# A hybrid decoder layer on one core: the mixer's steps are recorded in another order

## The chip, the core and the metric

The kernel runs on one core of a Trainium2 chip. A core has a matrix engine (TensorE, PE in the profile; its weight loads are PEld), three engines for elementwise work (VectorE or DVE, ScalarE or ACT, GpSimd or POOL) and a queue that issues transfers (SyncE or SP). Each engine works through its own instruction queue in order; semaphores tie the queues together. The metric is the time of one execution on the device in microseconds.

## What is computed

One decoder layer on a sequence of 512 tokens with 1024 features, all in float32: half a gated feed-forward step (2816 hidden), a mixer of windowed attention (16 query heads, 2 key heads, 64 each, window 128) and a 31-tap depthwise convolution, another half feed-forward step, and a gated per-layer embedding. The body of the reference:

```python
x = x + 0.5 * swiglu(rmsnorm(x, ffn1_norm[i]), ffn1_wgu[i], ffn1_wdown[i])
h = rmsnorm(x, mix_norm[i])
z = h @ w_in[i]
zq, zk, zv, zc, zg = [z[..., offs[j]:offs[j + 1]] for j in range(len(SPLIT_SIZES))]
...
q = partial_rope(q, cos, sin)
k = partial_rope(k, cos, sin)
a = sliding_window_attention(q, k, v, sinks[i]) @ attn_proj[i]
ca, cb = jnp.split(zc, 2, axis=-1)
u = ca * jax.nn.sigmoid(cb)
u = causal_depthwise_conv(u, dw_w[i], dw_b[i])
c = jax.nn.silu(layernorm(u, conv_ln_g[i], conv_ln_b[i])) @ conv_proj[i]
ga, gb = jnp.split(zg, 2, axis=-1)
merged = jax.nn.sigmoid(ga) * a + jax.nn.sigmoid(gb) * c
x = x + merged @ w_out[i]
x = x + 0.5 * swiglu(rmsnorm(x, ffn2_norm[i]), ffn2_wgu[i], ffn2_wdown[i])
e = rmsnorm(p[i] @ ple_proj[i], ple_norm[i])
gate = jax.nn.sigmoid(rmsnorm(x, ple_gate_norm[i]) @ ple_gate_w[i])
x = x + gate * e
```

Here `swiglu` is silu of one half of a product times the other half, times the second weight; queries and keys are normed per head ahead of the rotation.

## The kernel before

Activations are held with features on the 128 partitions and the 512 tokens along the free axis, so a 1024 x 512 activation is eight tiles of 128 x 512. Each float32 product is made of three matmuls in a reduced format: every operand is split into a high part (`_h`, `whi_`), rounded by ACT, and a low part (`_l`, `wlo_`), the rest, subtracted by DVE or POOL; `mm3` issues low weight by high activation, high by high, and high by low. So a projection of eight feature tiles (`proj`) is 24 matmuls, into one of the eight banks of PE's accumulator memory. Weights come in pieces of 128 x 1024 (512 KB), each loaded by SP, split by ACT and by DVE or POOL.

The mixer is written as a set of steps, each a function that records its instructions. The letters of `ORDER` name them: K keys and values; Q0 and Q1 the queries of the first and the second half of the heads; a*c* and b*c* the two convolution projections (`ca`, `cb`) of channel tile *c*, b with the sigmoid gate `sg`, the gated input `u` and the 31 taps of the convolution (products `ct` of ACT summed by POOL into `y` for some channel tiles, chained operations `cz` of DVE for the others); A*n*, E*n* and V*n* scores, softmax and values, where *n* = 4g + t stands for half g and block t of 128 tokens, so that A5 makes `qTp1_1`, `qT1_1` and `sc1_1`; g*o* the attention gate (`ga`, `sga`), h*o* the convolution's output gate (`gb`, `sgb`), p*o* the attention projection (`ap`); L the layer norm of the convolution (`ln_mb`, `ln_v_cs`, `ln_v_sp`, then Silu `y` and its parts `cv_h`, `cv_l`); e0 and e1 the per-layer embedding (products `e`, copies `es`, squares `ple_sq`, and with the last of them the sum `ple_cs` and spread `ple_sp` of its norm). Behind the steps come the convolution's projection `cp`, the output projection `wo` and FFN2 (`f_` in the trace).

Scores work thus: four PE transposes put a block's queries `zq` into a bank `qTp`, ACT rounds it to `qT_h`, DVE makes `qT_l` from both, and 12 matmuls follow, whose first one reads `qT_l`. Softmax: ACT takes exponentials with row sums `den`, POOL adds the sink, DVE inverts, POOL and ACT scale the blocks `s`. Values: eight transposes `pT`, splits `p_h` and `p_l`, masked copies `po`, products `o`, their sum `of` in a fixed layout, and its split into `oT`. Keys: PE transposes the four blocks `zk` into `kTp` after rotation and scaling on DVE and POOL.

The order in the queues is not that of the code. Line 40's `ORDER` only sets the order in which steps are recorded. `plan` then runs five rounds of `deadlines` and `simulate`, a model of the five engines with a cost for each kind of instruction. PE works through groups of matmuls (a projection is one) in the recorded order, and may pull forward a ready one of the next ten (`WINDOW`); the other engines take the ready instruction that is due first, and an instruction is due by when PE wants its result. For later rounds the groups are sorted by when they started. What the round with the shortest model time gives is issued, every engine's instructions sorted by their modelled start. All of them are issued by one line, 1522 in the profile, so groups are told by the names of their tiles. Part of the model is a cost of 1.28 us where ACT changes its function table, with `SETS = {"Exp": "e", "Sigmoid": "s", "Silu": "s"}`: the model counts Sigmoid and Silu as one table, and the built program has a table load between them.

Of the kernel before, what the change touches and what calls it, by code (L numbers as in the profile page):

```python
# [37 lines left out]


ORDER = """  # L40
K0 a0 b0 a1 Q0 A0 b1 a3 a2 A1 b2 E0 E1 b3 A2 E2 a4 V0 A3 a5 E3 V1 b4 Q1 V2 b5
V3 A5 a7 A6 g5 h7 A4 E5 A7 E6 E4 V6 g3 a6 E7 g0 V5 b6 V4 g4 g6 V7 h1 g2 h4 b7
g1 p0 p2 g7 p3 L0 p4 h3 p7 h2 p5 p1 e0 e1 p6 h5 h0 h6
"""
POOLCH = (0, 2, 4)
WARM = 9
# [1575 lines left out]
```

## Time and profile before

| | |
|---|---|
| median of three runs | 1172.97 us (1172.74 to 1175.81) |
| profiled execution | 1174.18 us, its span 1172.4 us |
| granted PE clock, mean of the span | 0.999 of full |
| busy: PE / PEld / DVE / ACT / POOL | 1161.6 / 1029.6 / 973.4 / 639.7 / 456.2 us |
| loads of ACT's function table | 18 of 1.28 us each |
| transfers | 115.30 MB, 98 GB/s on average |

Read the page from the busy times to the chain that ended last, then the waits of the engine that the chain names, then the windows of the stretch that the change touches, and only then the timeline of single places. FFN1 runs to about 354 us, the mixer's steps to about 690, where `cp` begins, and FFN2's first products stand at about 800. In a timeline row an instruction's duration runs from its start to its end; in a row of matmuls each begins before the one ahead has ended, so what a group costs is told from start to start.

### The profile page before, as it was taken

The numbers are of one execution on the slowest core, as the hardware profiler recorded it, in microseconds if no ns is written. First come the engines' busy times: TensorE is split into PE (matmuls) and PEld (weight loads), VectorE is DVE, ScalarE is ACT, GpSimd is POOL, SyncE is SP. The second block draws the span as 40 slices with busy tenths as digits, with TensorE's granted clock in tenths as the row PEclk, the third lists the DMA queues.
The fourth block names the chain that finished last, engine by engine and source line by source line (L and its number), as shares of the span: only waits on it lengthen the run. The fifth ranks groups of instructions, "written<-read, shape, count | busy, mean of one in ns | idle before, by whom it ended". The sixth has DMA issues, their size and how long they took to land.

```text
span 1172.4 us, 17962 instructions
## 1 busy us (share of the span) xinstructions
PE 1161.6 (99%) x6740; PEld 1029.6 (88%) x6740; DVE 973.4 (83%) x1481; ACT 639.7 (55%) x1139; POOL 456.2 (39%) x418
## 2 busy tenths in 40 slices
PE   9999999999999999999999999999999999999998
PEld 7898899889988888878888888889988999899886
DVE  8995799679886898999999786678966997599885
ACT  8552455335545579979865573545541555245542
POOL 2430465033303987887898600104402440122000
PEclk9999999999999999999999999999999999999999
DMA  7422323342233221312223233332333223331331
GB/s 226 146 85 96 126 75 106 99 136 76 82 104 100 90 91 37 108 55 72 76 89 106 88 94 93 105 96 102 107 104 132 74 86 100 121 127 41 104 108 72
DMA packets 37815, 115.30 MB, mean 98 GB/s; under 512 B 4704, under 2 KB 9440, under 8 KB 37728
## 3 DMA queue, kind: packets, MB, share of 16 engines
q1 hardware_dynamic: 37584, 114.12, 31.0%
q8 instruction: 53, 0.87, 0.3%
q14 instruction: 34, 0.28, 0.1%
q10 hardware_dynamic: 144, 0.03, 0.0%
HBM read 112.04 MB, written 2.10 MB: 97 GB/s over the span
## 4 chain that ended last, share of the span: by engine, by line
PE 94%; ACT 2%; DVE 2%; POOL 1%; issue 1%; DMA 0%; SPq 0%; DVEq 0%; ACTq 0%
PE f_d L1522 20%; PE ap L1522 4%; PE ga L1522 4%; PE pg L1522 4%; PE cp L1522 4%; PE wo L1522 4%; PE ca L1522 3%; PE gb L1522 3%; PE cb L1522 3%; PE f_u L1522 2%; PE f_g L1522 2%; PE q1b L1522 2%; PE q0b L1522 2%; PE sc L1522 2%; PE f_u14b L1522 1%; PE f_u20b L1522 1%
## 5 line engine op out<-in xcount | busy, mean ns | idle before, releaser
L1522 POOL TENSOR_TENSOR f_s<-raw_wgu,raw_wgu 128x512 f32<-128x512 f32 x51 | 86.6, 1710 | 345.5 <-DMA raw_wgu<-in_wgu 115.6
L1522 POOL TENSOR_TENSOR y<-y,ct 128x507 f32<-128x507 f32 (+27 forms) x90 | 119.1, 1343 | 6.2 <-ACT ct L1522 4.6
L1522 ACT ACTIVATE whi_wgu<-raw_wgu 128x1024 fp32r<-128x1024 f32 (+1 forms) x93 | 76.2, 834 | 81.5 <-PE f_d L1522 29.5
L1522 DVE TENSOR_TENSOR wlo_wgu<-raw_wgu,whi_wgu 128x1024 fp32r<-128x1024 f32 (+1 forms) x93 | 105.1, 1140 | 7.8 <-ACT whi_wgu L1522 7.3
L1522 DVE SCALAR_TENSOR_TENSOR cz<-u,dww,cz 128x504 f32<-128x504 f32 (+25 forms) x145 | 104.7, 732 | 2.3
L1522 ACT ACTIVATE whi_wd<-raw_wd 128x1024 fp32r<-128x1024 f32 (+1 forms) x48 | 47.4, 987 | 103.9 <-PE f_d L1522 84.6
L1522 DVE TENSOR_TENSOR f_d<-f_d,f_n_rb 128x512 f32<-128x512 f32 x48 | 33.4, 697 | 75.8 <-PE f_d L1522 75.8
L1522 DVE TENSOR_TENSOR f_wl<-f_s,f_wh 128x512 fp32r<-128x512 f32 x72 | 71.4, 1012 | 1.5 <-ACT f_wh L1522 1.0
L1522 POOL TENSOR_TENSOR f_s<-raw_wgu,f_s 128x512 f32<-128x512 f32 x31 | 52.3, 1694 | 51.6 <-DVE f_us L1522 20.6
L1522 DVE TENSOR_TENSOR wlo_wgu<-f_s,whi_wgu 128x512 fp32r<-128x512 f32 x80 | 66.3, 863 | 6.0 <-ACT whi_wgu L1522 5.8
L1522 ACT ACTIVATE whi_wgu<-f_s 128x512 fp32r<-128x512 f32 x80 | 46.6, 625 | 32.4 <-PE f_d L1522 8.9
L1522 ACT ACTIVATE ct<-u,dww 128x505 f32<-128x505 f32 (+28 forms) x90 | 58.2, 701 | 2.2 <-DVE u L1522 2.1
L1522 ACT ACTIVATE f_wh<-f_s 128x512 fp32r<-128x512 f32 x72 | 43.6, 626 | 26.6 <-DVE f_s L1522 12.9
L1522 POOL TENSOR_TENSOR f_s<-f_s,raw_wgu 128x512 f32<-128x512 f32 x31 | 49.2, 1594 | 20.8 <-DVE f_s L1522 6.0
L1522 DVE TENSOR_TENSOR wlo_wd<-raw_wd,whi_wd 128x1024 fp32r<-128x1024 f32 (+1 forms) x48 | 54.1, 1128 | 3.8 <-ACT whi_wd L1522 3.6
L1522 ACT ACTIVATE f_gs<-f_gs 128x512 f32<-128x512 f32 x44 | 27.6, 629 | 34.8 <-DVE f_gs L1522 34.4
L1522 POOL TENSOR_TENSOR f_t<-x 128x256 f32<-128x256 f32 x8 | 6.5, 807 | 86.8 <-DVE x L1522 81.6
L1522 DVE SCALAR_TENSOR_TENSOR x<-f_d,x 128x512 f32<-128x512 f32 x48 | 32.9, 689 | 1.4
L1522 DVE TENSOR_TENSOR f_s<-raw_wgu,raw_wgu 128x512 f32<-128x512 f32 x25 | 32.9, 1319 | 0.0
L1522 ACT ACTIVATE s<-s,m,q_r 128x128 f32<-128x128 f32 x64 | 31.0, 491 | 0.5 <-DVE m L1522 0.4
L1522 ACT ACTIVATE whi_wzc<-raw_wzc 128x1024 fp32r<-128x1024 f32 x16 | 17.0, 1061 | 22.3 <-issue 8.4
L1522 ACT ACTIVATE whi_wzg<-raw_wzg 128x1024 fp32r<-128x1024 f32 x16 | 17.1, 1069 | 16.9 <-PE ga L1522 5.0
(1621 smaller groups left out, 4525.3 us busy)
## 6 DMA issues: line engine op xcount, KB each, us to landing
raw_wgu<-in_wgu SPq DMA_DIRECT2D x80, 512.0 KB, 3.7
raw_wd<-in_wd SPq DMA_DIRECT2D x32, 512.0 KB, 3.5
raw_wzc<-in_wzc SPq DMA_DIRECT2D x16, 512.0 KB, 3.6
raw_wzg<-in_wzg SPq DMA_DIRECT2D x16, 512.0 KB, 3.6
raw_wd<-in_wd SPq DMA_DIRECT2D x16, 384.0 KB, 3.1
raw_wgu<-in_wgu SPq DMA_DIRECT2D x32, 128.0 KB, 2.9
raw_wq<-in_wq SPq DMA_DIRECT2D x8, 512.0 KB, 3.6
raw_wap<-in_wap SPq DMA_DIRECT2D x8, 512.0 KB, 3.6
```

The lines of the kernel that those rows point to most:

```text
L1522: getattr(engines[op.eng], op.what)(*a, **k)
```

## The change

Three lines of `ORDER` are replaced. Every step is still recorded once, each step's instructions are the same, and nothing else in the code changes. K0 stays first, Q0 and Q1 stay about where they were; convolution steps of tiles 3, 5 and 2 change places, values V1 are recorded ahead of E2, A6 comes ahead of A5, and at the end g, h and p steps are mixed in another way, with L and the two e steps ahead of h0 and p7.

```
 ORDER = """
-K0 a0 b0 a1 Q0 A0 b1 a3 a2 A1 b2 E0 E1 b3 A2 E2 a4 V0 A3 a5 E3 V1 b4 Q1 V2 b5
-V3 A5 a7 A6 g5 h7 A4 E5 A7 E6 E4 V6 g3 a6 E7 g0 V5 b6 V4 g4 g6 V7 h1 g2 h4 b7
-g1 p0 p2 g7 p3 L0 p4 h3 p7 h2 p5 p1 e0 e1 p6 h5 h0 h6
+K0 a0 a1 b0 Q0 A0 a3 b1 E0 a2 A1 E1 b3 a5 A2 V1 a4 E2 b2 V0 A3 E3 b4 Q1 V2 A6
+h7 V3 E6 b5 a7 A5 g5 A4 E5 E4 A7 V5 V6 g3 g6 a6 b6 h1 V4 g4 E7 b7 g0 V7 h3 h4
+p0 g2 g1 h2 g7 p2 p3 h6 p5 p6 p1 L0 p4 h5 e0 e1 h0 p7
 """
```

The first place is PE's queue at the second half's first scores. Before, the two clusters of transposes stand together, and the values of the block o0_3 stand between them and sc1_1:

```order
L1522 MATMUL o0_2_1_5503<-po0_2_1l_5455,v2_4083 128x512
L1522 MATMUL qTp1_1_5515<-ident_72,zq1_1_5394 128x128 x4
L1522 MATMUL qTp1_2_5522<-ident_72,zq1_2_5401 128x128 x4
L1522 MATMUL o0_3_0_5532<-p0_3_0_h_5450,v2_4083 128x512
L1522 MATMUL o0_3_0_5532<-p0_3_0_l_5467,v2_4083 128x512
L1522 MATMUL o0_3_0_5532<-po0_3_0h_5465,v3_4091 128x512
L1522 MATMUL o0_3_0_5532<-po0_3_0l_5490,v3_4091 128x512
L1522 MATMUL o0_3_1_5540<-p0_3_1_h_5457,v2_4083 128x512
L1522 MATMUL o0_3_1_5540<-p0_3_1_l_5475,v2_4083 128x512
L1522 MATMUL o0_3_1_5540<-po0_3_1h_5505,v3_4091 128x512
L1522 MATMUL o0_3_1_5540<-po0_3_1l_5513,v3_4091 128x512
L1522 MATMUL sc1_1_0_5555<-kzh_4314,qT1_1_l_5546 128x512
```

After, qTp1_1 stands behind those values, and a projection of 24 matmuls (ga5) follows it up to sc1_1:

```order
L1522 MATMUL o0_3_1_5642<-po0_3_1h_5571,v3_4091 128x512
L1522 MATMUL o0_3_1_5642<-po0_3_1l_5584,v3_4091 128x512
L1522 MATMUL qTp1_1_5657<-ident_72,zq1_1_5415 128x128 x4
L1522 MATMUL ga5_5662<-mix_h0_h_3680,wlo_wzg10_5544 128x512
L1522 MATMUL ga5_5662<-mix_h0_h_3680,whi_wzg10_5520 128x512
L1522 MATMUL ga5_5662<-mix_h0_l_3687,whi_wzg10_5520 128x512
```

The transposes qTp1_2 moved the other way: they stand ahead of pT0_3 and 24 matmuls of ca7 in the same manner, and sc1_2 now comes ahead of sc1_1.

The second place is ACT's queue ahead of the convolution's projection cp0, where `y` with `g_all` is a Silu and `sgb` a Sigmoid. Before, from the sixth Silu on:

```order
L1522 ACTIVATE y5_6054<-y5_6054,g_all_68 128x512
L1522 ACTIVATE cv4_h_7353<-y4_5188 128x512
L1522 ACTIVATE y6_6270<-y6_6270,g_all_68 128x512
L1522 ACTIVATE ple_rh_7369<-ple_r_7357 128x4
L1522 ACTIVATE cv5_h_7371<-y5_6054 128x512
L1522 ACTIVATE whi_wcp1_7378<-raw_wcp1_7221 128x1024
L1522 ACTIVATE y7_6611<-y7_6611,g_all_68 128x512
L1522 ACTIVATE cv6_h_7388<-y6_6270 128x512
L1522 ACTIVATE cv7_h_7395<-y7_6611 128x512
L1522 COPY ple_rb_7402<-ple_sp_7385 128x512
L1522 ACTIVATE whi_wcp2_7406<-raw_wcp2_7238 128x1024
L1522 ACT_TABLE_LOAD
```

After, from the fourth cv_h on:

```order
L1522 ACTIVATE whi_wcp1_7325<-raw_wcp1_7168 128x1024
L1522 ACTIVATE y4_5248<-y4_5248,g_all_68 128x512
L1522 ACT_TABLE_LOAD
L1522 ACTIVATE sgb0_7308<-sgb0_7308 128x512
L1522 ACT_TABLE_LOAD
L1522 ACTIVATE y5_5717<-y5_5717,g_all_68 128x512
L1522 ACTIVATE cv4_h_7351<-y4_5248 128x512
L1522 ACTIVATE y6_6285<-y6_6285,g_all_68 128x512
L1522 ACTIVATE cv5_h_7366<-y5_5717 128x512
L1522 ACTIVATE cv6_h_7370<-y6_6285 128x512
L1522 ACTIVATE y7_6845<-y7_6845,g_all_68 128x512
L1522 ACTIVATE whi_wcp2_7385<-raw_wcp2_7238 128x1024
```

sgb0's Sigmoid, which stood behind the last Silu and its load before, stands between the fifth Silu and the sixth now, with a load on each side; ple_rh and ple_rb stand behind cv7_h, and whi_wcp2 ahead of it. PE's groups around this place, before: ln_v_cs, ap6, gb5, ln_v_sp, ple_cs, gb0, gb6, ple_sp, cp0, cp1. After: ln_v_cs, e0 to e4, ln_v_sp, e5 to e7, gb0, ap7, ple_cs, cp0, cp1, ple_sp.

The third place is ACT's queue at FFN2's first gate, where `f2_gs0` is FFN2's first Silu and the COPY reads the bank of f_g2a (the names there have f2_ for f_). Before:

```order
L1522 ACTIVATE whi_wgu22_6_8291<-f2_s1_2_0_8215 128x512
L1522 ACTIVATE whi_wgu22_6_8291<-f2_s1_2_1_8220 128x512
L1522 ACT_TABLE_LOAD
L1522 ACTIVATE f2_gs0_8294<-f2_gs0_8294 128x512
L1522 COPY f2_gs2_8314<-f2_g2a_8287 128x256
```

After:

```order
L1522 ACTIVATE whi_wgu22_5_8249<-f2_s0_2_1_8202 128x512
L1522 ACTIVATE whi_wgu22_6_8291<-f2_s1_2_0_8215 128x512
L1522 ACTIVATE whi_wgu22_6_8291<-f2_s1_2_1_8220 128x512
L1522 ACTIVATE f2_gs0_8294<-f2_gs0_8294 128x512
L1522 COPY f2_gs2_8314<-f2_g2a_8287 128x256
```

The load is gone from this place; in all there are 14 in the program after and 18 before.

## Rows read from the trace of the kernel before

**Rows 1.** The page: PE's busy time, and the chain that ended last by engine.
```profile
PE 1161.6 (99%) x6740; PEld 1029.6 (88%) x6740; DVE 973.4 (83%) x1481; ACT 639.7 (55%) x1139; POOL 456.2 (39%) x418
...
PE 94%; ACT 2%; DVE 2%; POOL 1%; issue 1%; DMA 0%; SPq 0%; DVEq 0%; ACTq 0%
```

**Rows 2.** PE's waits: who waited for whom, us in total, times, longest.
```profile
PE sc L1522 <- DVE qT_l L1522: 2.0, 1, 2.0
...
PE f_g2a L1522 <- ACT f_gs L1522: 0.6, 1, 0.6
PE ple_sp L1522 <- DVE ple_dgl L1522: 0.6, 1, 0.6
...
PE kTp L1522 <- POOL zk L1522: 0.2, 1, 0.2
```

**Rows 3.** Windows, 400 to 600 us: length, busy PE, PEld, DVE, ACT, POOL, clock.
```profile
400.00:600.00 200.00, 197.99 (x933) 164.87 (x932) 189.03 (x316) 169.50 (x358) 170.71 (x201) 1.00 0.24 74
```

**Rows 4.** Timeline at the scores: start, duration, what, [idle before and releaser].
```profile
498.60 3.50 DVE L1522 TENSOR_TENSOR wlo_wzg<-raw_wzg,whi_wzg 128x1024 fp32r<-128x1024 f32 x1
...
501.93 1.04 PE L1522 MATMUL qTp<-ident,zq 128*128 128x128 f32 x8
502.02 3.28 DVE L1522 SCALAR_TENSOR_TENSOR cz<-u,dww,cz 128x501 f32<-128x501 f32 x5
...
506.05 1.29 DVE L1522 TENSOR_TENSOR qT_l<-qTp,qT_h 128x512 fp32r<-128x512 f32 x2
...
506.80 0.50 PE L1522 MATMUL sc<-kzh,qT_l 128*128 128x512 f32 x1 [2.01 <-DVE qT_l L1522]
```

**Rows 5.** The chain that ended last, 655 to 692 us: start, length, what.
```profile
665.78 5.61 PE ap L1522 x24
671.39 5.44 PE gb L1522 x24
676.83 0.45 PE ln_v_sp L1522 x2
677.28 0.79 PE ple_cs L1522 x8
```

**Rows 6.** Timeline of ACT, with one row of PE, ahead of cp0.
```profile
678.34 0.63 ACT L1522 ACTIVATE sgb<-sgb 128x512 f32<-128x512 f32 x1
678.99 1.28 ACT L1522 ACT_TABLE_LOAD   x1
680.29 1.52 ACT L1522 ACTIVATE y<-y,g_all 128x512 f32<-128x512 f32 x2
...
689.93 0.50 PE L1522 MATMUL ple_sp<-ple_dgl,ones_r 128*128 128x512 f32 x1 [0.59 <-DVE ple_dgl L1522]
...
690.12 1.14 ACT L1522 ACTIVATE cv_h<-y 128x512 fp32r<-128x512 f32 x2
...
692.71 1.28 ACT L1522 ACT_TABLE_LOAD   x1
```

**Rows 7.** Timeline of ACT at FFN2's first gate.
```profile
804.79 1.28 ACT L1522 ACT_TABLE_LOAD   x1
```

**Rows 8.** Timeline: the last square of e (ACT), ln_v_sp's last operand (DVE).
```profile
666.36 0.73 ACT L1522 ACTIVATE ple_sq<-e 128x512 f32<-128x512 f32 x1
...
671.46 0.67 DVE L1522 TENSOR_TENSOR ln_v_dgl<-ident,ln_v_cs 128x512 fp32r<-128x512 f32 x1
```

**Rows 9.** The chain that ended last, 440 to 475 us: sc0_2 and pT0_2.
```profile
444.41 2.72 PE sc L1522 x12
...
471.19 0.44 PE pT L1522 x4
```

**Rows 10.** Timeline of POOL at the third softmax.
```profile
465.58 2.40 POOL L1522 TENSOR_TENSOR wlo_wq<-raw_wq,whi_wq 128x1024 fp32r<-128x1024 f32 x1
468.13 1.29 POOL L1522 TENSOR_TENSOR sg<-sg,mix_n_rb 128x512 f32<-128x512 f32 x1 [0.15 <-ACT sg L1522]
469.40 1.07 POOL L1522 TENSOR_SCALAR s<-s,den 128x128 f32<-128x128 f32 x3
```

## The prediction

> **What bounds the kernel now.** The page comes first. TensorE (PE) is busy 99% of the span, and 94% of the chain that ended last is PE [rows 1]; its granted clock is 1.00, the higher of its levels, in the moved stretch [rows 3]. So the time is the sum of PE's instructions plus the gaps between them, and a change that moves no clock can win only gaps. The view of PE's waits says which there are: seven, and of these four lie in the moved code or hang on it, 2.0 at the scores, 0.6 at ple_sp, 0.6 at f_g2a and 0.2 at kTp [rows 2]; the other three stand in code that keeps its place. That is 3.4 us, a ceiling for the gain; a loss has none. (Each gap costs about 0.2 more than the view says, since the matmul behind it takes 0.50 to its end [rows 4], where in a row of 24 one starts each 5.44 / 24 = 0.23 [rows 5].) The windows say which engine could become late: VectorE (DVE), busy 189 of 200 us between 400 and 600, with ScalarE (ACT) and GpSimd (POOL) at 170 [rows 3].
>
> The profiled execution took 1174.18 us with a span of 1172.4, so 1.8 us lie outside the span; it is 1.2 us above the median of the runs, 1172.97. I make the sum as a difference within the span and put it on the median.
>
> **The change part by part.** Every step issues the same instructions in both kernels, and PE's rows are the same in number; nothing but table loads and waits is added or removed. What moves is rows of all five queues between the end of FFN1 and the first products of FFN2.
>
> *1. Scores of the second half.* Before, the transposes qTp1_1 and qTp1_2 at 501.93 are followed by the eight o0_3 matmuls alone, 8 × 0.23 = 1.8 us of cover, and sc1_1 waits 2.01 us: DVE works through five convolution steps (3.28 us from 502.02) and an output sum, and only at 506.05 makes qT_l [rows 4]. After, qTp1_2 stands ahead of pT0_3 and a projection of 24 matmuls (ca7), and qTp1_1 ahead of the 24 of ga5; such a projection takes 5.44 us [rows 5]. From the transposes to the release it was 506.80 − 501.93 = 4.9 us before, with a DVE that had no pause. 5.44 covers that. Gain 2.0 + 0.2 = 2.2; the lower end is 1.2, if DVE is 1.5 us later than it was there.
>
> *2. ple_sp.* Its second matmul waits 0.59 us at 689.93 [rows 6]: 0.8 with the restart. After, ple_cs stands right ahead of cp0 and ple_sp behind cp1, so 2 × 5.44 us and what cp0 waits (part 6) lie between. From ple_cs's end to that matmul it was 678.07 to 689.93 = 11.9 us before [rows 5, 6], because the chain's small DVE operations are strung between large ones; the cover of 10.9 plus 2.1 is just more. Gain 0.8; 0 to 1 of a new wait goes into the range.
>
> *3. FFN2's first gate.* Before, the mixer's last load is of Sigmoid's table (692.71 [rows 6]), so FFN2's first Silu needs one of 1.28 us at 804.79 [rows 7], ahead of the copy that frees f_g2a's bank, and f_g2a waits 0.6 [rows 2]. After, y5's Silu has the last load of the mixer and none stands here; the copy comes 1.28 earlier. Gain 0.6 + 0.2 = 0.8.
>
> *4. kTp.* The third of the four transposes waits 0.2 for POOL's zk [rows 2]. After, the pieces of work for wlo_wq0 and sg0 stand behind the k chain, and the zk operations come earlier. Gain 0.2 + 0.2 = 0.4; the lower end is 0.
>
> *5. Fewer clusters.* A projection behind a cluster of narrow matmuls takes 5.61 where 5.44 is usual [rows 5]; behind transposes it is the same kind of start. There are 13 clusters of transposes after instead of 15: 2 × 0.12, 0.2.
>
> Gains together: 2.2 + 0.8 + 0.8 + 0.4 + 0.2 = 4.4 us.
>
> *6. The convolution's norm, ahead of cp0: a loss.* Before, ACT loads Silu's table at 678.99 and runs the eight Silus (y) and eight cv_h copies with a weight copy and ple_rh among them; Sigmoid's load comes behind, at 692.71. From 680.29 to the last cv_h's end, 690.12 + 1.14, it is 11.0 us [rows 6], some 9.9 without the other two. After, sgb0's sigmoid stands behind y4, among the Silus, with a load on each side, and two weight copies (whi_wcp1, whi_wcp2) stand ahead of cv7_h. From the first load on it is then 1.3 + 9.9 + 2 × 1.0 + 0.5 + 2 × 1.3 = 16.3.
>
> When does that start, and when is PE there? I count from ln_v_cs's first matmul. PE after: ln_v_cs 1.7, thirty matmuls of e 6.9, ln_v_sp 0.45, eighteen of e 4.1 (13.2 so far), gb0 and ap7 5.45 each, ple_cs 0.8: cp0 starts at 24.9 and wants cv7_h for its 22nd matmul, at 29.7, and cv7_l for its 24th. ACT after: it must first copy and square e7 (two operations of up to 0.73 that overlap, 1.0 [rows 8]), 14.2, then whi_wcp0, 15.2; plus 16.3 is 31.5, and DVE's cv7_l some 0.65 later, 32.1. PE waits 31.5 − 29.7 = 1.8 for cv7_h and some 0.3 for cv7_l: **2.1 us**. Before, cv7_h was there at 691.3 and cp0's 22nd matmul came at about 695: no wait. ln_v_sp has 6.9 us of cover, where its last operand was ready at 671.46 + 0.67 = 672.1 [rows 8], 6.6 behind ln_v_cs's end and with a weight piece in between; no wait. The ends of the 2.1: 0.5 if ACT is 1.6 us ahead of my count, 3.5 if one or two large operations stand ahead of it.
>
> The Trainium skill (ScalarE: Activation LUTs, What ACT_TABLE_LOAD costs) gives about 1283 ns for the load and about 1380 ns of drain, 2.66 us for a switch; by it the three loads would add some 4.1 us to this wait. Here sgb's sigmoid ends at 678.97, the load of 1.28 starts at 678.99 and the first y 0.02 behind its end [rows 6]: the load agrees, and no drain shows.
>
> *7. The third softmax: a smaller loss.* pT0_2 came 24.0 us behind the end of sc0_2 before (444.41 + 2.72 to 471.19 [rows 9]); after, 18.6 us of matmuls lie between. POOL's last scaling of its s blocks ended at 470.5 before, 0.7 ahead of PE, behind a weight piece of 2.40 and a gate product of 1.29 [rows 10]; both stand in that chain after, too. Worked forward from the exponentials it is ready 18.2 to 20.6 us behind sc0_2: a wait of 0 to 2. I take 0.5, nearer the low end, since POOL ran other additions ahead of its scalings before. The other transposes and value products keep 1 us or more.
>
> *8. All else.* Groups of FFN1 and FFN2 that swap places had no wait there: 0 to 0.5, taken as 0.1.
>
> Sum: −4.4 + 2.1 + 0.5 + 0.1 = −1.7. On the median 1172.97 − 1.7 = **1171.3 us**.
>
> **The rivals.**
> - *A. No wait at cp0.* If ACT is ahead of my count there, or PE later, part 6 falls to zero and the gains stand nearly alone: −4.4 + 0.5 = −3.9, 1169.1. For: ACT is the least busy of the three in the windows [rows 3]. Against: e7 and its square pin ACT to 14.2.
> - *B. The gaps only move.* A PE queue that is some 2 us earlier meets its producers 2 us earlier, and what is won comes back in small waits between 400 and 660: −4.4 + 2.1 + 2.3, 1173.0. For: DVE's 189 of 200. The change then does to the queues what it says, and nothing to the end.
> - *C. DVE falls behind: slower.* One operation of DVE took 3.50 us, wlo_wzg at 498.60, and ran up against the gap of part 1; its queue is in order [rows 4]. After, the same work stands in another sequence. If qT_l, an output sum or p_l comes more than 5.44 us behind its transposes, each such place costs up to the 2.2 of part 1. It decides from four places on: −1.7 + 4 × 2.2 = +7.1, 1180. For: DVE's share. Against: of all places before only the one with 1.8 us of cover waited, none with 5.44.
> - *D. Loads as dear as with a drain.* Each of part 6's three loads then takes 1.4 more: −1.7 + 4.1 = +2.4, 1175.4. The Trainium skill (same section) says so; against it stands the 0.02 in [rows 6].
>
> **How the numbers follow.** The forecast 0.46 (1169.7 to 1173 by its own ends), A 0.17, B 0.21, C 0.13, D 0.03. The runs of the kernel before lie up to 3 us apart, so under 0.3% (3.5 us) can't be told from no change: 1169.5 to 1176.5. The forecast, B and D lie within it, A under it, C over it: faster 0.17, same 0.70, slower 0.13. The range takes in A and D, 1168.7 to 1176.0, and leaves out C and what lies beyond A.
>
> **What would show it.** Right: no sc, ple_sp or f_g2a among PE's waits; 14 table loads instead of 18, two of them around one sigmoid between the fifth and the sixth Silu; one PE wait of 1.5 to 3 us in the cp rows, on cv_h or cv_l; for part 7 a pT wait under 1 us near 465. Wrong: cp0 without a wait (then A); several waits of 1 us or more on DVE between 400 and 600 (then C); more than 0.1 us behind a load (then D). PE's busy sum and its clock must stay as they are; else the account itself is wrong.

## The result, and the profile after

The changed kernel takes 1178.84 us (median; 1178.49 to 1180.76) where the kernel before takes 1173.03 (1172.74 to 1175.81) beside it: a ratio of 1.0048, 95% interval 1.0037 to 1.0059. It is slower by half a per cent, above the range that was predicted. The profiled execution took 1179.03 us with a span of 1177.2, 4.8 more than the one of before.

PE's busy time and the chain that ended last, from the page after, beside [rows 1]:

```profile
PE 1164.1 (99%) x6740; PEld 1028.7 (87%) x6740; DVE 976.4 (83%) x1478; ACT 635.4 (54%) x1135; POOL 457.4 (39%) x421
...
PE 90%; ACT 5%; DVE 4%; issue 1%; DMA 0%; POOL 0%; SPq 0%; DVEq 0%; ACTq 0%; POOLq 0%
```

PE issues the same 6740 matmuls, and its share of the chain has fallen from 94 to 90%; ACT's and DVE's have risen. ACT has four instructions fewer, the four table loads that are gone (14 for 18). PE's busy sum has grown by 2.5 us, although its matmuls and its mean clock (0.999) are the same; where that comes from is told with part 6 below. PE's waits after, beside [rows 2] (who waited for whom, us in total, times, longest):

```profile
PE sc L1522 <- DVE of L1522: 1.2, 1, 1.2
...
PE cp L1522 <- ACT cv_h L1522: 0.9, 2, 0.8
...
PE f_g18b L1522 <- DVE f_g18a L1522: 0.7, 1, 0.7
PE ga L1522 <- DVE s L1522: 0.6, 1, 0.6
PE f_g6b L1522 <- DVE wlo_wgu L1522: 0.5, 1, 0.5
PE f_g6a L1522 <- DVE wlo_wgu L1522: 0.5, 1, 0.5
```

All four waits of before that lay in the moved code are gone: the scores' for qT_l, ple_sp's, f_g2a's and kTp's. New ones stand at a score group (released by DVE's `of`, not by qT_l), at cp, at a ga, and, against the prediction, in both FFNs. Windows of FFN1's end of pairs, the stretch of [rows 3] and FFN2's early pairs, first after, then the two FFN windows before (length, busy PE, PEld, DVE, ACT, POOL, clock):

```profile
280.00:300.00 20.00, 19.33 (x161) 19.13 (x160) 19.51 (x29) 10.32 (x19) 10.08 (x6) 1.00 0.23 85
400.00:600.00 200.00, 198.12 (x929) 164.20 (x928) 188.47 (x315) 162.45 (x352) 171.29 (x201) 1.00 0.24 74
...
830.00:850.00 20.00, 18.77 (x152) 18.16 (x151) 18.55 (x19) 9.40 (x17) 13.96 (x9) 1.00 0.21 65
```

```profile
280.00:300.00 20.00, 20.00 (x169) 20.00 (x169) 16.91 (x26) 10.83 (x19) 7.07 (x5) 1.00 0.24 79
...
830.00:850.00 20.00, 20.00 (x169) 20.00 (x168) 19.86 (x30) 11.76 (x21) 9.79 (x6) 1.00 0.24 77
```

The clock is the higher level in all three, as before. Between 400 and 600 hardly anything has changed in sum. In the other two PE was busy for all 20.00 us before and has gaps now, and POOL is busier: 10.08 and 13.96 us for 7.07 and 9.79.

Where the 4.8 us came from is read by laying the two traces over each other: the start of a PE group after, less the start of the same group before.

| up to this group | after − before, us | the step |
|---|---|---|
| FFN1's f_u16b | +0.34 | start-up |
| f_g20a, FFN1 | +1.26 | **+0.92**, pair 18/20 of FFN1 |
| q0b | +0.73 | −0.53, kTp's wait is gone |
| wo | +3.25 | **+2.52**, the mixer |
| behind f_g2a | +2.47 | −0.78, FFN2's first gate |
| the last projection `pg` | +4.79 | **+2.32**, pairs 4 and 6 of FFN2 |

In the mixer PE's groups stand in another sequence, so its 2.52 are told from the time between a group's start and the next one's: gone are 2.27 at the scores and 0.86 at ple_sp; new are 1.51 at sc0_3, 0.83 at eight transposes ahead of a ga, twice some 0.2 at pT and 2.77 at cp0 and cp1 (13.65 for 10.88). That makes 2.4 of the 2.52.

**FFN2.** DVE's, POOL's and PE's rows at pairs 4 and 6, after (start, duration, what, [idle before and releaser]):

```profile
839.47 1.98 DVE L1522 TENSOR_TENSOR wlo_wgu<-raw_wgu,whi_wgu 128x1024 fp32r<-128x1024 f32 x1
...
842.81 4.54 DVE L1522 TENSOR_TENSOR wlo_wgu<-raw_wgu,whi_wgu 128x1024 fp32r<-128x1024 f32 x2
...
835.30 3.37 POOL L1522 TENSOR_TENSOR f_s<-raw_wgu,raw_wgu 128x512 f32<-128x512 f32 x2 [3.70 <-issue]
838.63 3.98 POOL L1522 TENSOR_TENSOR f_s<-f_s,raw_wgu 128x512 f32<-128x512 f32 x2
842.57 3.70 POOL L1522 TENSOR_TENSOR f_s<-raw_wgu,raw_wgu 128x512 f32<-128x512 f32 x2
...
845.18 0.38 PE L1522 MATMUL f_g6b<-f_h_h,wlo_wgu 128*128 128x256 f32 x1 [0.53 <-DVE wlo_wgu L1522]
```

The same place before:

```profile
832.82 0.69 DVE L1522 TENSOR_TENSOR f_s<-raw_wgu,raw_wgu 128x512 f32<-128x512 f32 x1
...
838.31 1.98 DVE L1522 TENSOR_TENSOR wlo_wgu<-raw_wgu,whi_wgu 128x1024 fp32r<-128x1024 f32 x1
...
833.64 3.33 POOL L1522 TENSOR_TENSOR f_s<-f_s,raw_wgu 128x512 f32<-128x512 f32 x2 [3.02 <-ACT f_uc L1522]
836.92 4.52 POOL L1522 TENSOR_TENSOR f_s<-raw_wgu,raw_wgu 128x512 f32<-128x512 f32 x2
```

These `f_s` are sums of two weight halves, and each is made by DVE or by POOL as the planner decides. Before, DVE made one of them itself in 0.69 us, and POOL four. After, POOL makes six without a pause from 835.30 to 846.27, and DVE's weight splits stand beside them. Such a split of 128x1024 takes 1.21 us with POOL idle (283.42 in FFN1, below), 1.98 at 839.47 beside POOL's sums, and 2.27 each in the pair at 842.81. PE, which had run without a gap here, now waits for the splits.

**FFN1.** The same picture at pair 18, after:

```profile
283.20 2.32 DVE L1522 TENSOR_TENSOR wlo_wgu<-raw_wgu,whi_wgu 128x1024 fp32r<-128x1024 f32 x1
285.44 1.51 DVE L1522 TENSOR_TENSOR f_us<-f_us,f_gs 128x256 f32<-128x256 f32 x1
...
287.47 0.42 DVE L1522 TENSOR_TENSOR f_g18a<-f_g18b,f_gs 128x256 f32<-128x256 f32 x1
...
282.81 3.85 POOL L1522 TENSOR_TENSOR f_s<-raw_wgu,f_s 128x512 f32<-128x512 f32 x2 [4.46 <-ACT whi_wgu L1522]
```

and before:

```profile
283.42 1.21 DVE L1522 TENSOR_TENSOR wlo_wgu<-raw_wgu,whi_wgu 128x1024 fp32r<-128x1024 f32 x1
284.56 0.43 DVE L1522 TENSOR_TENSOR f_g18a<-f_g18b,f_gs 128x256 f32<-128x256 f32 x1
...
289.29 2.12 POOL L1522 TENSOR_TENSOR f_s<-raw_wgu,f_s 128x512 f32<-128x512 f32 x1 [7.87 <-ACT f_a20h L1522]
```

Before, POOL's sum ran 6 us later, DVE had the stretch to itself, and f_g18a, which reads f_g18b's bank and so frees it, came at 284.56. After, two sums of POOL stand beside DVE's two operations. The four end one behind the other: the split needs 1.21 alone and 0.41 is usual for the product, but they take 2.32 and 1.51, and f_g18a comes at 287.47. PE waits 0.7 for it.

**Ahead of cp0**, ACT's rows after, beside [rows 6], with PE's at cp0's 22nd matmul:

```profile
688.87 1.28 ACT L1522 ACT_TABLE_LOAD   x1
690.16 0.63 ACT L1522 ACTIVATE sgb<-sgb 128x512 f32<-128x512 f32 x1
690.81 1.28 ACT L1522 ACT_TABLE_LOAD   x1
692.11 0.81 ACT L1522 ACTIVATE y<-y,g_all 128x512 f32<-128x512 f32 x1
...
696.75 0.61 ACT L1522 ACTIVATE cv_h<-y 128x512 fp32r<-128x512 f32 x1
...
697.42 0.50 PE L1522 MATMUL cp<-cv_h,wlo_wcp 128*128 128x512 f32 x1 [0.78 <-ACT cv_h L1522]
```

The last cv_h ends at 697.36, 31.9 us behind ln_v_cs's start (665.45); the prediction counted 31.5. An ACT operation follows each load 0.01 to 0.02 us behind its end, so no drain shows in these rows, and rival D's price is not paid.

**At sc0_3**, where no wait was expected, DVE and PE after:

```profile
462.74 1.46 DVE L1522 SCALAR_TENSOR_TENSOR cz<-u,dww,cz 128x495 f32<-128x495 f32 x2
464.11 1.26 DVE L1522 TENSOR_TENSOR wlo_wq<-raw_wq,whi_wq 128x1024 fp32r<-128x1024 f32 x1
465.33 2.12 DVE L1522 TENSOR_TENSOR of<-o,of 64x512 f32<-64x512 f32 x3
...
466.07 0.50 PE L1522 MATMUL sc<-kzh,qT_l 128*128 128x512 f32 x1 [1.16 <-DVE of L1522]
```

The scores' operands are there; what is missing is the bank. PE's accumulator has eight, and the one that this sc0_3 group needs is held by a value product until DVE has added it to `of`; that sum stands behind two convolution steps and a weight split. The planner's own assignment of banks agrees: it gives sc0_3's second group the bank of o0_1_0.

**At the ga that waits** (0.58 at 525.50; ga3 in the program), the releaser is DVE's copy into `s`, and the assignment gives ga3 the bank of sc1_1_0, which that copy reads last. What makes the copy late shows in the rows ahead of it, DVE's and POOL's:

```profile
523.32 1.78 DVE L1522 TENSOR_TENSOR m<-m,sinks_n 128x8 f32<-128x8 f32 x1
...
522.70 2.37 POOL L1522 TENSOR_TENSOR wlo_wzg<-raw_wzg,whi_wzg 128x1024 fp32r<-128x1024 f32 x1
```

The DVE operation has eight columns and at its shortest takes 0.11 us in this trace. Here it takes 1.78 and ends at 525.10, when POOL's split ends (525.07): DVE and POOL stand in each other's way in the mixer too. No run took the two apart there.

### The profile page after: what moved, and what is told of

Its sections match the earlier page's. It is cut to its first block, busy times and chain, and to the rows that moved or that the text cites. A ratio compares the mean times of both kernels' runs of the same rounds, so it can differ in the third digit from the quotient of the medians.

```text
span 1177.2 us, 17947 instructions
## 1 busy us (share of the span) xinstructions
PE 1164.1 (99%) x6740; PEld 1028.7 (87%) x6740; DVE 976.4 (83%) x1478; ACT 635.4 (54%) x1135; POOL 457.4 (39%) x421
## 4 chain that ended last, share of the span: by engine, by line
PE 90%; ACT 5%; DVE 4%; issue 1%; DMA 0%; POOL 0%; SPq 0%; DVEq 0%; ACTq 0%; POOLq 0%
PE f_d L1522 20%; PE ga L1522 4%; PE pg L1522 4%; PE wo L1522 4%; PE cp L1522 3%; PE ap L1522 3%; PE gb L1522 3%; PE ca L1522 3%; PE cb L1522 3%; PE f_u L1522 2%; PE f_g L1522 2%; PE q0b L1522 2%; PE q1b L1522 2%; DVE wlo_wgu L1522 1%; PE sc L1522 1%
## 5 line engine op out<-in xcount | busy, mean ns | idle before, releaser
L1522 POOL TENSOR_TENSOR y<-y,ct 128x509 f32<-128x509 f32 (+28 forms) x90 | 117.2, 1326 | 5.9 <-ACT ct L1522 4.6
L1522 DVE SCALAR_TENSOR_TENSOR cz<-u,dww,cz 128x510 f32<-128x510 f32 (+27 forms) x145 | 102.4, 731 | 1.2
L1522 ACT ACTIVATE ct<-u,dww 128x511 f32<-128x511 f32 (+28 forms) x90 | 58.4, 701 | 1.6 <-DVE u L1522 1.5
L1522 DVE TENSOR_TENSOR f_s<-raw_wgu,raw_wgu 128x512 f32<-128x512 f32 x24 | 30.0, 1251 | 0.0
```

Source lines behind the costliest of these rows:

```text
L1522: getattr(engines[op.eng], op.what)(*a, **k)
```

## The experiments

Twelve runs follow; the eleventh is the kernel before once more. Most of the kernels are spliced: each engine's sequence is taken in three parts, FFN1, the mixer, and FFN2 with what follows, each from the kernel after (A) or before (B), and further edits work on the joined sequence. The cuts lie in FFN1's last products and inside wo, at points by which both kernels have issued the same instructions. In the expectations, T is the reading of the table above, that the FFNs and the mixer each cost their share, and P that POOL's sums beside DVE's splits are the cause in the FFNs.

**1 and 2. Mixer alone, FFNs alone.** The first takes the mixer from after and both FFNs from before; the second the reverse.

```diff
+PARTS = ('B', 'A', 'B')
```

```diff
+PARTS = ('A', 'B', 'A')
```

> The mixer's rows stand as in the changed kernel, both feed-forward stretches as in the kernel before (the queues were spliced at the end of FFN1 and in the middle of FFN2's first groups). Theory T (by the two traces, FFN1 lost 1.3 us and FFN2 2.3 us, apart from the mixer, which lost 2.5 less 0.5 at kTp and 0.8 at FFN2's first gate): about +1.2 over the kernel before, 1174.2 us, no waits near 286 and 841 us. Rival R (one stretch's gaps only travel to the next; the total belongs to the mixer's order): it stays near the changed kernel, 1178 us.

> The opposite splice: the mixer's rows as in the kernel before, both feed-forward stretches as in the changed one. Theory T: +3.6 over the kernel before, 1176.6 us, with the waits at 286 to 289 and 841 to 856 us of the changed kernel. Rival R: about 1173, as before.

Mixer alone: 1175.71, beside 1173.13 for before, ratio 1.0014 (1.0006 to 1.0023). FFNs alone: 1176.83, ratio 1.0029 (1.0018 to 1.0040). 2.6 + 3.7 = 6.3, where the whole change costs 5.8. The mixer's steps, which are all that the change names, account for less than half; more comes from FFN1 and FFN2, in which ORDER names nothing. The planner's shortest round was another one: the third of its five instead of the second. When `plan` is run for both ORDERs, FFN2's queues have the same sequence in the same round whichever ORDER is given, so there the round alone makes the difference; FFN1's PE sequence differs in every round. In these runs of `plan` the model gives 1169.8 us for the new ORDER and 1172.3 for the old, so it forecast a gain too. The mixer alone came out 1.5 above its theory's +1.2, which was read against the one profile of before with the long wait at the scores (part 1 below). In the second kernel FFN1 costs 0.93 and FFN2 1.99, with the same waits at f_g18b, f_g6b and f_g6a.

**3. One sum moved to POOL, in the kernel before.** Before, DVE makes one f_s of FFN2's early pairs itself; here POOL does, and nothing else differs.

```diff
+    for o in prog.ops:
+        if o.flex and o.writes[0].vt.name == "f2_s0_6_0":
...
+            o.eng = "POOL"
```

> The kernel before with one instruction moved: the addition s0_6_0 of FFN2's pair 6 (128 x 512) runs on POOL instead of DVE, as in the changed kernel. Theory P (a POOL addition that runs beside DVE slows both, and DVE's late weight pieces hold up PE): PE waits on wlo_wgu appear at 838 to 848 us, 0.7 to 2.3 us longer. Rival Q (the order of DVE's own rows makes the loss): DVE has 0.6 us less to do, no new wait, 1173.

1175.05 beside 1173.13, ratio 1.0016 (1.0007 to 1.0025). DVE, POOL and PE there, and behind them DVE's row at that place in the kernel before:

```profile
831.32 3.49 DVE L1522 TENSOR_TENSOR f_a00l<-f_us,f_a00h 128x512 fp32r<-128x512 f32 x2
...
827.99 3.12 POOL L1522 TENSOR_TENSOR f_s<-raw_wgu,raw_wgu 128x512 f32<-128x512 f32 x2 [3.81 <-ACT whi_wgu L1522]
831.08 3.18 POOL L1522 TENSOR_TENSOR f_s<-f_s,raw_wgu 128x512 f32<-128x512 f32 x2
...
837.16 0.39 PE L1522 MATMUL f_g4a<-f_h_h,wlo_wgu 128*128 128x256 f32 x1 [0.71 <-DVE wlo_wgu L1522]
```

```profile
831.43 1.47 DVE L1522 TENSOR_TENSOR f_a00l<-f_us,f_a00h 128x512 fp32r<-128x512 f32 x2
```

The two f_a00l took 1.47 us in the kernel before and take 3.49 beside POOL's two sums; f_g4a waits twice, 1.1 in all, and FFN2 becomes 2.1 us longer. DVE gave away 0.69 us of work and lost 2.02 on its next pair.

**4 and 5. One sum moved to DVE, in the kernel after.** First the same one in FFN2, back to where it was before; then, in FFN1, one of the two that stood beside DVE at 283 (before, POOL made that one too, but at 289.29).

```diff
+    for o in prog.ops:
+        if o.flex and o.writes[0].vt.name == "f2_s0_6_0":
...
+            o.eng = "DVE"
```

```diff
+    add = find("tensor_tensor", "f1_s3_18_1", "POOL")
...
+    add[0].eng = "DVE"
```

> The changed kernel with the same addition moved back from POOL to DVE, all other rows as they are. Theory P: the FFN2 loss of 2.3 us shrinks to under 1, 1177 us. Rival Q: it stays at 2.3 or grows by 0.7, 1178.8 to 1179.5.

> The changed kernel with one addition of FFN1's pair 18 (s3_18_1, 128 x 512) on DVE instead of POOL. Theory P (POOL additions that run beside DVE's late rows cost FFN1 its 1.3 us): the 0.7 us wait of f_g18b on DVE goes or falls under 0.3, 1.0 us won, 1177.8. Rival Q (DVE's own order, in which f_g18a stands behind a weight piece and f_a20l): DVE has 0.7 more to do ahead of it, the wait stays or grows, 1178.8 or more.

1177.25 beside 1173.13, ratio 1.0030 (1.0016 to 1.0043), and 1178.04 beside 1173.35, ratio 1.0034 (1.0023 to 1.0045). FFN2's new cost falls from 2.32 to 0.86 in the first; in the other kernel FFN1's falls from 0.92 to nothing, and the wait at f_g18b is gone. So P holds in FFN2 from both sides, with the sum put there and taken away, and in FFN1 from one side. What is left of FFN2's cost, 0.86, still has a wait at f_g6a, and no run tried what makes it.

**6. sgb0's Sigmoid behind the last cv_h**, in the mixer-alone kernel.

```diff
+    sig = [o for o in find("activation", "sgb0", "ACT")][0]
+    behind(sig, find("activation", "cv7_h", "ACT")[0])
```

> The kernel with the changed mixer and the feed-forwards of before (1175.7), and sgb0's Sigmoid moved behind the last cv_h, so that the eight Silus stand behind one table load; the last load of the mixer is Sigmoid's again. If two loads and the Sigmoid are what PE waits for at cp0: cp's 2.7 us of loss go (3.1 us of ACT work leave the path), f_g2a's 0.8 comes back in FFN2, 1173.8. If cp0 waits for something else (DVE's queue, the weight copies): 1176.5. If a load cost 2.66 us: ACT would be 5.8 us earlier, which shows in the trace at cv7_h.

1174.12 beside 1173.35, ratio 1.0006 (0.9996 to 1.0015). The waits at cp are gone, and from FFN1's f_u16b to wo it is 2.6 us less than in the mixer-alone kernel: that is part 6's place and size. The Sigmoid's load is the mixer's last again, and f_g2a waits 0.6 again, as before: part 3's mechanism, from the other side (2.6 − 0.8 is the 1.8 by which the two medians, each against its own before, differ). Both kernels have 14 loads. Among the Silus, the Sigmoid and the two loads around it cost 2.6; behind them, its one load shows no wait, and the Silu load that FFN2 then needs costs 0.8 at f_g2a.

**7 and 8. The banks.** In the mixer-alone kernel DVE's three `of` go ahead of the weight split that stood before them (`lo`); so that they can, the Sigmoid of sg4 on ACT (`sig`), its product on POOL (`mul`) and DVE's u4 move back. The eighth kernel adds the edit of the sixth and a Silu of one column on ACT during cp, whose result nothing reads, to have FFN2's table loaded early.

```diff
+    behind(sig, last)
+    behind(mul, max(s, key=lambda o: o.start))
+    behind(lo, max(ofs, key=lambda o: o.start))
+    behind(u4, max(ofs, key=lambda o: o.start), 2)
...
```

```diff
+    small = prog.tile("table2", [P, 1], F32, "c")
+    prog.scalar.activation(small, V(ones)[:, 0:1], AF.Silu)
+    load = prog.ops[-1]
...
+    behind(load, find("activation", "mg1h", "ACT", ("sga4",))[0])
```

> The kernel with the changed mixer and the feed-forwards of before (1175.7), and at 464 us the four output copies of ACT ahead of the table load for sg4, DVE's output sums ahead of the weight piece wlo_wq5, and sg4's product on POOL behind the scalings. If sc0_3 waits for a bank that those sums free: the 1.5 us there fall to 0.3, 1174.5. If it waits for another thing (qT_l, PE's own order): 1175.7 or more.

> Both moves together and a Silu of one column (its result unused) on ACT during cp, which fetches Silu's table while ACT is idle, so that FFN2's first gate finds it loaded. If the ledger holds, 1175.7 - 2.7 - 1.2 = 1171.8, under the kernel before by 1.3 us. If the gaps only travel: 1174 to 1176.

1178.77, ratio 1.0037 (1.0023 to 1.0052), and 1176.22, ratio 1.0015 (1.0006 to 1.0025), both beside 1173.35; the 1174.5 and 1171.8 that were expected did not come. The wait at sc0_3 is gone, so it was for the bank that the sums free; but u4, which the edit put behind the sums, frees the bank of ca4, and the next pT waits for that. As a repair the edit failed. The PE row, and two windows of the seventh kernel:

```profile
469.39 1.97 PE L1522 MATMUL pT<-ident,s 128*128 128x128 f32 x8 [2.85 <-DVE u L1522]
...
468.00:472.00 4.00, 2.60 (x10) 2.43 (x11) 3.22 (x7) 2.32 (x7) 1.25 (x2) 0.55 0.40 131
472.00:476.00 4.00, 4.00 (x12) 3.17 (x11) 3.00 (x5) 3.05 (x5) 3.91 (x4) 0.59 0.00 0
```

In the windows at the end of this gap of 2.85 us and behind it the granted clock is 0.55 and 0.59, a mean of both levels, and the cb of 24 matmuls behind takes 7.53 us, where it took 5.57 in the mixer-alone kernel. In the eighth kernel f_g2a's wait is gone and FFN2's first gate is 0.77 shorter: the load was what it waited for.

**9. The kernel before, mended in three places**, with its own ORDER: the one-column Silu; ple_dgl ahead of y7's product on DVE; qT1_1_l and qT1_2_l ahead of the last three convolution steps.

```diff
+    behind(find("tensor_tensor", "y7", "DVE")[-1], find("tensor_tensor", "ple_dgl", "DVE")[0])
...
+    lo = find("tensor_tensor", "qT1_2_l", "DVE")[0]
...
+    for n, o in enumerate(cz):
+        behind(o, lo, n + 1)
```

> The kernel before with three places mended and ORDER left as it was. (1) A Silu of one column, whose result nothing reads, stands on ACT during cp, so that FFN2's first Silu finds its table loaded; if the load was what f_g2a waited for (theory), its wait of 0.6 goes and the stretch shortens by 0.7 to 0.8; if the bank came late for another reason (rival), the wait stays. (2) DVE makes ple_dgl ahead of y7's product; theory: ple_sp's wait of 0.6 goes, 0.6 to 0.9. (3) DVE makes qT1_1_l and qT1_2_l ahead of the last three convolution steps that stood before them; theory: the scores' wait goes, 0.4 to 2.0 by the run. Sum by theory: -1.6 to -3.6, about 1171 on the median of before's runs near 1173.2. Rival (gaps only move): DVE's later steps, pushed back by 0.7 to 2, make PE wait elsewhere, and the time stays at 1173.

1172.78 (1172.45 to 1173.65) beside 1172.85 (1172.03 to 1176.68), ratio 0.9993 (0.9984 to 1.0002), and not the 1171 that was expected. f_g2a's wait went, and 0.4 of ple_sp's 0.6. At the scores the wait only changed its reason: two waits for a bank that `of` frees, 0.66 and 0.35. The first two edits held their theory, the third its rival.

**10. The changed mixer with the Sigmoid late and the one-column Silu**, FFNs of before.

```diff
+    behind(sig, find("activation", "cv7_h", "ACT")[0])
...
+    load = prog.ops[-1]
...
+    behind(load, find("activation", "mg1h", "ACT", ("sga4",))[0])
```

> The changed mixer between the FFNs of before, with sgb0's Sigmoid behind cv7_h as in the earlier run with that edit alone (1174.1), and the one-column Silu of the first kernel of this call on ACT during cp, its result unused. Theory: f_g2a's wait of 0.6, which came back when the Sigmoid's load became the mixer's last, goes again, and nothing else moves: 1174.1 - 0.75 = 1173.4. Left in the mixer are then the scores' wait for a bank (1.1) and ga's (0.6), against the waits of before that the new ORDER removes (0.4 to 2.0 at the scores, 0.6 at ple_sp). Rival: the extra load delays a product of cp's epilogue, 1174 or more.

1173.25 (1172.71 to 1174.88), ratio 1.0001 (0.9992 to 1.0010), as expected to 0.2. With the table loads placed well and the FFNs left alone, the new sequence of the mixer is worth nothing either way that this measurement can tell.

**11. The kernel before, profiled again.**

> The kernel before once more, unchanged, for a second profile. If its wait at the second half's first scores differs from run to run (theory), it is nearer 0.4 than 2.0 here, with a span of some 1171 and a time near 1173; if the 2.0 belongs to the kernel (rival), it stands here again.

The expectation failed: this execution took 1176.38 with a span of 1174.6, and the wait for qT_l was 2.0 again. It showed something else. Of the 2.2 us beyond the first profile 0.55 are start-up and 1.6 arise at one place, behind that wait. The windows there, and the second of them in the first profile:

```profile
504.00:508.00 4.00, 2.00 (x8) 1.35 (x8) 3.94 (x7) 2.74 (x6) 4.00 (x9) 0.96 0.68 242
508.00:512.00 4.00, 4.00 (x12) 3.10 (x11) 3.45 (x7) 2.27 (x6) 2.01 (x3) 0.61 0.04 12
```

```profile
508.00:512.00 4.00, 4.00 (x19) 3.29 (x19) 3.94 (x11) 3.94 (x11) 2.04 (x4) 1.00 0.03 8
```

The clock fell to 0.61 behind a gap of 2.00 us. In the first profile it stayed at 1.00 behind one of 2.01.

**12. The kernel before with the first two edits of the ninth.** Against the ninth:

```diff
-    lo = find("tensor_tensor", "qT1_2_l", "DVE")[0]
...
-    for n, o in enumerate(cz):
-        behind(o, lo, n + 1)
```

> The kernel before with two of the three edits of the earlier run that mended three places: the one-column Silu on ACT during cp (its result unused) and ple_dgl ahead of y7's product on DVE; DVE's order at the second half's scores is left as it was. In that earlier run f_g2a's wait went (0.77 to the next group) and 0.4 of ple_sp's 0.6, yet the median stayed at 1172.8. Theory: the third edit ate it, since the scores then waited 1.0 for a bank where in most executions of the kernel before they wait 0.4 for qT_l (wlo_wzg of 1.9 us there, and 3.5 in the ones that wait 2.0); without it the median is 1172.9 - 1.2 = 1171.7. Rival: the gains at ple_sp and f_g2a come back later, in FFN2 or behind it, and the median stays at 1172.8. In the profile wlo_wzg near 499 tells which of the two waits to look for at the scores: about 0.4 with 1.9, about 2.0 with 3.5.

1175.14 (1172.01 to 1175.38) beside 1174.81 (1173.16 to 1176.63), ratio 0.9999 (0.9990 to 1.0008). The profiled execution is the shortest of the study, 1172.01, and there everything stood as expected: f_g2a and ple_sp 1.2 us shorter, and a wait of 0.5 at the scores behind a split of 1.90. But seven of its eleven executions took 1174.84 to 1175.38, all with a mean granted clock of 0.997 or 0.998, and the other four at most 1173.5, at 0.999 or 1.000. So the median of 1171.7 was missed, and on the median the edits do not beat the kernel before. That does not clear the third edit of the ninth kernel: from FFN1's f_u16b to wo the profile is 1.91 shorter than the first one of before here and 1.09 there, with the split at 1.9 in both, so there the edit did cost 0.8. But with it no execution went over 1173.65. Whether its two short waits in place of a long one kept the clock up there was not tried apart.

Why the scores' wait is 2.0 in one execution and 0.5 in another shows in DVE's and POOL's rows. First the eleventh kernel (the kernel before), then the twelfth:

```profile
499.14 3.49 DVE L1522 TENSOR_TENSOR wlo_wzg<-raw_wzg,whi_wzg 128x1024 fp32r<-128x1024 f32 x1
...
499.92 0.47 POOL L1522 TENSOR_TENSOR zq<-zq,q_w 128x128 f32<-128x128 f32 x1
500.33 0.64 POOL L1522 TENSOR_SCALAR_AFFINE_SELECT po_1h<-p_h 128x512 fp32r<-128x512 f32 x1
500.92 0.64 POOL L1522 TENSOR_SCALAR_AFFINE_SELECT po_1l<-p_l 128x512 fp32r<-128x512 f32 x1
```

```profile
499.16 1.90 DVE L1522 TENSOR_TENSOR wlo_wzg<-raw_wzg,whi_wzg 128x1024 fp32r<-128x1024 f32 x1
...
499.96 1.43 POOL L1522 TENSOR_TENSOR zq<-zq,q_w 128x128 f32<-128x128 f32 x1
```

Counted from the start of the span, both splits start within 0.02 us of each other. In one, POOL's string goes through (0.47, 0.64, 0.64) and DVE's split ends 1.1 behind it; in the other POOL's zq is held up by a microsecond (1.43 for 0.47) and the split ends 1.6 earlier. Which of the two gets through differs from execution to execution, and PE's wait with it.

## Why the prediction was wrong

**The step that failed is part 8, "all else"**: taken as 0.1, ends 0 to 0.5. With it fell the sentence ahead of the parts, that what moves lies between the end of FFN1 and the first products of FFN2. It measured 0.92 + 2.32 = 3.2 us in the profile, and the FFNs alone cost 3.7 on the median. The argument was that the swapped groups had no wait before. That was true, and it excluded nothing: they had no wait because PE had a lead there, and the change took the lead away on two other queues, not on PE's. DVE's share of the window 830 to 850 in the kernel before is 19.86 of 20.00; the prediction looked for a late DVE between 400 and 600 (rival C) and never asked the same of the FFNs. (In FFN1's window the share is 16.91, so it would not have told of that place.) It also treated which engine makes a sum as settled, though the change moved both sums that DVE made in FFN2's pair 6 to POOL.

**The bank waits of the mixer** were the second miss: 1.51 at sc0_3 and 0.83 ahead of a ga, both for a bank that DVE frees late. Parts 1 and 7 followed operands only. Rival C named the mechanism (an output sum too late on DVE) with 2.2 a place and four places; two came, at 1.5 and 0.8. That the ga's wait is of the same kind is read from its releaser and from the planner's banks; no run tried it.

**Part 7** (0.5 for pT0_2): the view of waits names none there; the group takes 1.01 us where eight transposes take 0.79 elsewhere, one of the two 0.2 above.

**Part 6** (2.1, ends 0.5 to 3.5) measured 2.77; the sixth kernel puts the Sigmoid away and gives 2.6 back. The wait stands where it was put, at cp0's 22nd matmul for the last cv_h (0.78), and in between for each late cv_h and cv_l; the count of ACT's work was 0.4 off. Here lies most of PE's longer busy sum, which the prediction wanted unchanged: of the 2.77 the view of waits shows 0.9, in two gaps. The rest stands between matmuls whose records still overlap (one begins 0.33 to 0.5 us behind the other instead of 0.23), and counts as busy. An unchanged busy sum was the wrong thing to ask for; the work is the same.

**Parts 1 to 4** came in the profile as counted: 2.27 at the scores for 2.2, 0.86 at ple_sp for 0.8, 0.78 at f_g2a for 0.8, 0.53 at kTp for 0.4. Part 1 was mis-sized for the median all the same: the 2.2 were taken from one execution, 1.2 us above the median. Where the split takes 1.9, the third and twelfth profiles show waits of 0.44 and 0.50, so there the gain is 0.7 or 0.8. That fits the medians lying 5.8 apart where the profiled executions lie 4.8. **Part 5** (0.2) was not measured by itself; projections behind clusters take 5.54 to 5.60 after and 5.54 to 5.57 before.

In sum, as the profile has it: forecast −1.7, measured +4.8. Of the 6.5 between them 3.1 are part 8, 2.3 the two bank waits, 0.7 part 6, 0.4 the pT's and 0.3 start-up, less 0.5 for part 7 and 0.2 for the gains; 0.4 are not assigned, part 5's 0.2 among them. The largest miss is a stretch that the prediction held to be untouched, but the sign does not hang on it: the mixer alone is 2.6 slower on the median (run 1), by the bank waits, by part 6, and by part 1's smaller gain. The forecast had the first at nothing, part 6 too small and part 1 too large.

## What to carry over

Where a planner or scheduler stands between the code and the queues, compare the queues everywhere, and price an untouched-looking stretch by the lead of its feeding engines, not by the waits it has. Count sums and splits on DVE and POOL that stand side by side as if one stood behind the other, and ask of each group on PE for its bank as well as for its operands. A gap's price belongs to an execution: look at a second profile before a single gap carries the sum.

## What the runs showed of the hardware

- DVE and POOL hold each other up. In FFN1 after, two sums of POOL (1.28 to 1.3 each where they are shortest) and two operations of DVE (1.21 and 0.41 alone) fill the 4.1 us from 282.81 to 286.95, which is near their sum of 4.2. The Trainium skill (SBUF — State Buffer, SBUF: two separate sides) says that a VectorE operation with two SBUF inputs and a GpSimd operation that reads SBUF exclude each other, and that the second to start is blocked until the first ends. The FFN rows agree, and so do the 1.78 us of an eight-column operation ahead of ga3. At 499 they show more: DVE's split was passed by several POOL instructions in a row in one execution (3.49) and got in ahead of one in another (1.90), with starts 0.02 us apart.
- The granted clock fell to a mean of 0.61, and to 0.55 and 0.59, behind PE gaps of 2.00 and 2.85 us, and the matmuls behind took 1.6 and 2.0 us longer than those of the same groups elsewhere. Behind another gap of 2.01 it stayed at 1.00. What decides is open.
- A table load on ACT costs 1.28 us, and the next operation starts 0.01 to 0.02 behind it; a one-column Silu is enough to move it to where ACT has time (0.77 or 0.78 won at FFN2's first gate).
